# Triangular substitution of a two-stream recurrence: two passes on 64 partitions, or one on 128

## The chip, the cores and the metric

The kernel runs on one core of a Trainium2 chip. The metric is device time in microseconds (us) of one execution. Before the change the median of three runs is 4465.26 us (4459.31 to 4469.98).

## The reference

Two blocks of a network run one after the other over 1024 tokens of 1024 features: a block of two layers (attention and gating, then a mixture of experts, each twice), and a second block with windowed attention, a linear recurrence over time and an MLP. The change touches only the recurrence of the second block. Per head (8 heads of 64 features) and per direction (forward and backward), with a state `S` of 64 by 64:

```python
def step(S, inp):
    r_t, w_t, kk_t, b_t, k_t, v_t = inp
    sa = jnp.einsum('bhvk,bhk->bhv', S, -kk_t)
    S = S * w_t[:, :, None, :] + sa[..., None] * b_t[:, :, None, :] + v_t[..., None] * k_t[:, :, None, :]
    y = jnp.einsum('bhvk,bhk->bhv', S, r_t) if emit else None
    return S, y

S, ys = lax.scan(step, S0, xs, reverse=reverse)
...
for d, rev in enumerate((False, True)):
    S_ctx, yc_d = wkv7_scan(S0, r_c, dec_c, kk_c, b_c, k_c, v_c, rev, update_ctx)   # 256 context tokens
    _, y_d = wkv7_scan(S_ctx, r_l, dec_l, kk_l, b_l, k_l, v_l, rev, True)           # 1024 tokens
    y_lat.append(y_d)
```

The outputs of both directions are added, normalised per head, and merged with the attention branch by two gates; an MLP follows.

## The kernel before

**The recurrence in chunks.** The kernel does not go token by token. It takes chunks of 64 tokens (`C = 64`). Inside a chunk the dependence of tokens on each other is a strictly triangular matrix `A` of 64 by 64 per head and direction, and the chunk needs `(I - A)^-1`. Two chunks of each direction make a group; there are 10 groups (2 over the context, 8 over the tokens). The 8 heads are cut into two streams of four heads (class `Stream`, `hs` = 0 and 1). So one stream in one group has 2 directions x 2 chunks x 4 heads = 16 matrices.

**One group of one stream, before.**
1. `ahead` loads the decayed operands (`AR`, `BKf`; `prepare`, L1866), multiplies them with each other on PE (`pairs`, L1890), masks the products into `MS` on DVE (L1892) and stores the triangles into DRAM as `A_d` (L1898, four stores).
2. `blocks` (L1924) reads back the 16 by 16 blocks on the diagonal of the 16 matrices, four each, so 64 blocks, one per partition (`NL`, L1929). It inverts them by substitution: for n = 1 to 15 one multiplication (L1936) and one reduction (L1938) on DVE, each on 64 partitions by at most 225 elements, each needing the one before. The result goes to DRAM twice, as it is and transposed (`X_d<-XL`, `X_d<-XC`, L1943).
3. `levels` loads the inverses back among zeros, by halves of the partitions (`XX`, `XT`, four loads, L1950), joins the blocks of 16 to 32 and to 64 by small matmuls (`invert`, L1969, L1979) and forms what the values add (`products`, L1920).
4. `finish` makes two steps (`step`, L2011): previous state in, outputs and next state out. From group n = 4 of the tokens on it also calls `output` (L2075), which normalises, transposes (L2105) and stores a finished tile.

So the blocks of 16 go through DRAM twice: `MS` to `A_d` to `NL`, then `XL`, `XC` to `X_d` to `XX`, `XT`. A set of blocks is one pass through step 2; before there are 20 sets (10 groups x 2 streams).

**What runs beside it.** `others` (L1310) yields the window's attention (tiles `wQ`, `wK`, `wP`) and the gates (`gh`, `gw`, products `psA<-gh..,gw..`, L138), piece by piece; `SHARES` says how many pieces follow each group. The recurrence is emitted with priority (`HP = 5000`). A scheduler then fixes one order of instructions per engine, and the engines run these orders as written: an instruction that waits holds all that stand behind it on its engine. All loads and stores of the recurrence go over the SP queue; the gates' loads go over POOL's. What comes after the recurrence is `merge` (tiles `yr`, `ya`).

**Order between the streams.** Before, the loop over the groups goes stream by stream: `ahead` of the next group, `finish` of this one, `levels` of the next one for stream 0, then all three for stream 1. The tiles of `blocks` and of `output` share buffers: `yg` stands in the buffer of `NL` and `XC` (tag `NX`), `yv` and `yrL` in that of `LL`, `ysq` and `yrH` in that of `prod`.

Of the kernel before, what the change touches and what calls it, by code (L numbers as in the profile page):

```python
# [43 lines left out]
class K:  # L44
    """Engines, pools and the few operations that every phase uses."""
# [14 lines left out]
    def after(s, eng):  # L60
        """Work to be queued behind the last instruction of an engine so far."""
        todo = s.nc.cur_bb.bb.instructions
        return s.tc.issue_after(next(x for x in reversed(todo) if x.engine == eng.engine))
# [13 lines left out]
    def banks(s, es, **n):  # L77
        """The eight banks of PSUM, by what they are for, until es closes."""
        old = dict(s.ps)
        s.count += 1  # L80
        p = s.pool(es, f"ps{s.count}", 1, space=PSUM)
        s.ps.update({tag: (p, m) for tag, m in n.items()})

        def back():
            s.ps = old

        es.callback(back)
# [20 lines left out]
    # float32 as the sum of two float32r parts, exact  # L108
# [9 lines left out]
    def row_max(s, pool, todo, mx):  # L118
        """Largest of scores + mask by rows, one column of mx each."""
# [5 lines left out]
    def to_rows(s, pool, cols, n, *dst):  # L125
        """The negatives of columns, one after the other in rows of partition 64."""
# [13 lines left out]
    def weights(s, raw, ring, src, shape, leng=None, queue=None):  # L140
        """A block of weights, loaded and split."""
# [11 lines left out]
    def rstd(s, ss, n, scale, eps, name):  # L153
        """(ss * scale + eps) ** -0.5, few elements per partition."""
# [6 lines left out]
    def bcast(s, pool, ap, n, name, parts=128, **kw):  # L161
        """A row of n values in DRAM on every partition."""
# [5 lines left out]
    def norm_pair(s, pool, xs, gb, outs, eps=EPS, gb2=None):  # L168
        """Two token tiles normalised over their 1024 features and scaled by gb (plus gb2)."""
# [11 lines left out]
    def transpose4(s, src, n=4):  # L181
        """Four [128, 128] blocks of a token tile, transposed into one PSUM bank."""
# [5 lines left out]
    def to_hT(s, src, hH, hL, t):  # L188
        """A token tile [128, 1024] into features by tokens, split."""
# [12 lines left out]
# ---------------------------------------------------------------- even mixer  # L202
# [4 lines left out]
def even_mixer(k, es_out, x_d, w, mod_d):  # L207
    """x_d: DRAM [1024, 1024]. w: DRAM inputs. Returns the output projection and what it takes. The second
    block's modulation goes by the way."""
# [42 lines left out]
def proj_tile(k, hH, hL, W, t, n):  # L252
    """h of token tile t times a block of weights given in chunks of two k-tiles."""
# [74 lines left out]
def even_project(k, es, w, raw, ring, hH, hL, q_d, k_d, v_d):  # L328
    """Queries, keys and values, rotated, in their two parts: q_d, k_d [part, head, feature, token], v_d [part, head,
    token, feature]."""  # L330
# [36 lines left out]
NQ = 4  # heads whose operands are on chip at a time  # L367
# [31 lines left out]
def even_head(k, p2, mb, mc, me, h, slot, q_d, k_d, v_d, a_d, r_d):  # L399
# [13 lines left out]
    # values, by tokens shifted by half a tile and by residue classes of 4  # L413
# [12 lines left out]
    with k.tc.high_priority(offset=HP):  # L426
        # row maxima of both key sets
# [28 lines left out]
    def attend():  # L456
# [21 lines left out]
        # band of 64 tokens to either side  # L478
# [3 lines left out]
        def pv(b, c, v, P):  # L482
            # one accumulation group per bank: what is not yet written is overwritten
# [25 lines left out]
        # dilations 4 and 16, within the residue classes of 4  # L509
# [16 lines left out]
def normalise(k, p2, O, r_row, dst, shape=None, more=None):  # L526
    """Rows 0..63 of O over its row 64 into DRAM. more adds to the row, spread over the partitions."""
# [12 lines left out]
class OutProj:  # L540
    """x + a @ w_out by token tiles; a: features by tokens in DRAM, one tile of 128 features each."""
# [40 lines left out]
# ---------------------------------------------------------------- mixture of experts  # L582
# [5 lines left out]
class Moe:  # L588
    """Expert choice over the tokens of x1; x_d gathers x1 and what the experts add to it."""

    def __init__(s, k, es, i, w, x_d):
# [8 lines left out]
        # the router takes the tokens before their norm: its weights by the norm's  # L600
# [38 lines left out]
    def rank(s, x, last):  # L639
        """The best of every expert so far and these: in order, but for the last time."""  # L640
# [9 lines left out]
        if s.best is not None:  # L650
            # the best of two lists: the one against the other from its end; then sorted
# [14 lines left out]
    def choose(s):  # L666
        """Which slot of which expert a token takes: those above the last of the best by their order, then the
        first of its equals."""
        k, p = s.k, s.p1
        # token number and gate in parts that bfloat16 carries exactly  # L670
# [19 lines left out]
        # how many up to a token, and how many above in all  # L690
# [16 lines left out]
    def gather(s, p, e):  # L707
        """The tokens of an expert, their numbers and gates."""
# [18 lines left out]
    def experts(s):  # L727
        k, w, i = s.k, s.w, s.i
        s.es.close()
        with ExitStack() as es:  # L730
# [11 lines left out]
            # in the order of use: the first products of an expert go ahead of the last of the expert before  # L742
# [65 lines left out]
# ---------------------------------------------------------------- odd mixer  # L808
# [31 lines left out]
def odd_mixer(k, es_out, x_d, w):  # L840
    """x_d: DRAM [1024, 1024]. w: DRAM inputs. Returns the output projection and what it takes."""
    a_d = [k.dram.tile([128, T], F32, name=f"a_do{i}") for i in range(8)]
    r_d = k.dram.tile([16, T], F32, name="r_d1")
    # operands of the attentions in their two parts, features by tokens, by heads or pairs of heads
# [25 lines left out]
def odd_proj(k, es, x_d, w, d):  # L870
# [23 lines left out]
    # ranks: queries, keys and values, rotary keys  # L894
# [27 lines left out]
    def heads(x, n, g, r, t):  # L922
        """Norms and rotations of n heads of a token tile."""
# [8 lines left out]
    def split_rows(src, dst, half, m):  # L932
        """Four token tiles' columns src(t) as features by tokens, split, into dst[part]."""
# [50 lines left out]
    # from the ranks to the heads  # L984
# [39 lines left out]
def odd_attention(k, es, d, a_d, r_d):  # L1024
# [13 lines left out]
    def head(n, h):  # L1038
# [25 lines left out]
        # row maxima of the scores, negated, into a row of the queries' operand  # L1064
# [41 lines left out]
# ---------------------------------------------------------------- second block  # L1106

TC = 256  # context tokens
C = 64  # tokens of a chunk of the recurrence
# [687 lines left out]
class Stream:  # L1797
# [32 lines left out]
    def ahead(s, ctx, n):  # L1830
# [5 lines left out]
        for i in range(2):  # L1836
            s.pairs(B, i)
# [631 lines left out]
```

## Time and profile before

| | before |
|---|---|
| median of 3 runs, us | 4465.26 (4459.31 to 4469.98) |
| span of the profiled execution, us | 4467.4 |
| PE busy, share of the span | 89% |
| DVE busy | 66% |
| ACT busy | 41% |
| POOL busy | 25% |
| first substitution to last one (L1936, L1938), us | 2781.7 to 3451.0 |

The span runs from the first to the last instruction of one profiled execution; it lies between the runs' times, and no other time of that execution is given. PE is TensorE, DVE VectorE, ACT ScalarE, POOL GpSimd, SP the queue that issues most DMAs. A busy PE is not a PE at its peak: the records of matmuls overlap. The recurrence stands in the stretch from 2760 to 3560 us.

### The profile page before, as it was taken

How to read it: one execution, taken by the hardware profiler on the slowest of the kernel's cores; microseconds unless marked ns; L12 is line 12 of the kernel's file. 1: busy time of each engine (PE TensorE's matmuls, PEld its weight loads, DVE VectorE, ACT ScalarE, POOL GpSimd, SP SyncE). 2: the span in 40 equal slices, each digit the busy share in tenths (PEclk: the TensorE clock that was granted, in tenths of full speed). 3: DMA queues.
4: the chain of work that ended last, by engine and by line, in shares of the span. 5: the costliest groups of instructions: out<-in, count | busy, mean ns of one | idle time of the engine just before them, and what ended most of it. 6: DMA issues, size and time to landing. Idle time of an engine off the chain costs nothing. (4 is left out here: it accounts for less than half of the span.)

```text
span 4467.4 us, 65652 instructions
## 1 busy us (share of the span) xinstructions
PE 3963.4 (89%) x24208; PEld 3233.3 (72%) x24208; DVE 2938.6 (66%) x5925; ACT 1815.5 (41%) x3066; POOL 1109.1 (25%) x1069
## 2 busy tenths in 40 slices
PE   7898995897978999689948997999988899999998
PEld 7797884775855666567737776777777678888887
DVE  8656658896678875879866793766677565332334
ACT  3223332675447775257634452333333432212212
POOL 2211212121213433112133363222244511101101
PEclk9998997999989999889968998989998999999999
DMA  5758435898267543569933446555756662111112
GB/s 163 228 170 187 110 112 186 304 367 279 82 189 176 116 102 93 188 238 365 329 111 118 148 148 181 138 142 137 166 145 147 190 210 88 57 48 48 49 55 85
DMA packets 568286, 714.12 MB, mean 160 GB/s; under 512 B 243636, under 2 KB 355332, under 8 KB 567964
## 3 DMA queue, kind: packets, MB, share of 16 engines
q1 hardware_dynamic: 467788, 510.50, 37.3%
q0 software_dynamic: 42480, 144.62, 11.9%
q10 hardware_dynamic: 57696, 54.80, 3.8%
q8 instruction: 191, 3.13, 0.3%
q14 instruction: 131, 1.07, 0.1%
HBM read 555.84 MB, written 153.53 MB: 159 GB/s over the span
## 5 line engine op out<-in xcount | busy, mean ns | idle before, releaser
L116 DVE TENSOR_TENSOR w_l<-w_raw,w_h 128x2048 fp32r<-128x2048 f32 (+5 forms) x336 | 592.2, 1769 | 194.1 <-ACT w_h L111 192.9
L111 ACT ACTIVATE w_h<-w_raw 128x2048 fp32r<-128x2048 f32 (+4 forms) x344 | 507.2, 1487 | 437.4 <-PE psO L138 254.5
L138 PE MATMUL psA<-w_h,hH 128*128 128x256 f32 (+3 forms) x896 | 292.6, 330 | 28.9 <-ACT w_h L111 13.7
L138 PE MATMUL psA<-w_l,hH 128*128 128x256 f32 (+3 forms) x896 | 292.6, 327 | 1.9 <-DVE w_l L116 1.7
L138 PE MATMUL psA<-w_h,hL 128*128 128x256 f32 (+3 forms) x896 | 291.3, 326 | 0.0
L116 POOL TENSOR_TENSOR uL<-relu,uH 128x512 fp32r<-128x512 f32 x64 | 82.6, 1291 | 571.9 <-ACT uH L111 571.9
L138 PE MATMUL psA<-w_h,xH 128*128 128x512 f32 x512 | 208.5, 409 | 11.6 <-ACT xH L111 8.8
L138 PE MATMUL psA<-w_l,xH 128*128 128x512 f32 x512 | 211.1, 412 | 7.1 <-DVE w_l L116 6.9
L138 PE MATMUL psA<-w_h,xL 128*128 128x512 f32 x512 | 206.1, 404 | 4.3 <-DVE xL L116 4.3
L138 PEld LDWEIGHTS psA<-w_h,hH 128*128 128x128 f32 x896 | 174.5, 196 | 41.6 <-ACT w_h L111 15.1
L2287 DVE TENSOR_TENSOR relu<-relu 128x512 f32<-128x512 f32 x64 | 44.3, 693 | 238.2 <-ACT relu L2286 238.2
L116 DVE TENSOR_TENSOR PL<-P,PH 128x512 fp32r<-128x512 f32 x192 | 171.1, 903 | 27.3 <-ACT PH L111 27.1
L138 PEld LDWEIGHTS psA<-w_l,hH 128*128 128x128 f32 x896 | 175.3, 196 | 10.4 <-DVE w_l L116 4.6
L138 PE MATMUL psA<-ghH,gwH 128*128 128x256 f32 x512 | 169.6, 331 | 14.5 <-DMA ghH<-hs_d 5.0
L138 PEld LDWEIGHTS psA<-w_h,hL 128*128 128x128 f32 x896 | 175.1, 195 | 5.3 <-issue 2.6
L805 POOL DMA_INDIRECT x_d<-yo,idx x32 | 69.8, 2182 | 421.5 <-ACT yo L804 417.5
L111 ACT ACTIVATE gwH<-gw 128x256 fp32r<-128x256 f32 x256 | 103.3, 414 | 163.1 <-PE psA L138 121.0
L138 PE MATMUL psA<-ghH,gwL 128*128 128x256 f32 x512 | 161.2, 315 | 1.3 <-POOL gwL L116 1.0
L138 PE MATMUL psA<-ghL,gwH 128*128 128x256 f32 x512 | 160.4, 313 | 0.0
L116 POOL TENSOR_TENSOR gwL<-gw,gwH 128x256 fp32r<-128x256 f32 x128 | 97.5, 765 | 248.3 <-ACT gwH L111 207.5
L111 ACT ACTIVATE PH<-P 128x512 fp32r<-128x512 f32 x256 | 154.5, 629 | 6.5 <-POOL PL L116 1.3
L116 POOL TENSOR_TENSOR PL<-P,PH 128x512 fp32r<-128x512 f32 x64 | 90.9, 1420 | 231.2 <-ACT PH L111 178.2
(654 smaller groups left out, 11896.8 us busy)
## 6 DMA issues: line engine op xcount, KB each, us to landing
w_raw<-in_moe_w_gate_dram SPq DMA_DIRECT2D x64, 1024.0 KB
w_raw<-in_moe_w_up_dram SPq DMA_DIRECT2D x64, 1024.0 KB
w_raw<-in_moe_w_down_dram SPq DMA_DIRECT2D x64, 1024.0 KB
gw<-in_w_in_t_dram POOLq DMA_DIRECT2D x64, 512.0 KB, 5.5
wada<-in_w_ada_dram POOLq DMA_DIRECT2D x48, 512.0 KB, 5.8
w_raw<-in_w_mlp_up_dram SPq DMA_DIRECT2D x16, 1024.0 KB
w_raw<-in_w_mlp_down_dram SPq DMA_DIRECT2D x16, 1024.0 KB
AR<-ar_d SPq DMA_DIRECT2D x40, 256.0 KB
```

Of the source, the lines that this page charges most:

```text
L111: s.a.activation(h, x, AF.Copy)
L116: (eng or s.v).tensor_tensor(l, x, f(h), op=ALU.subtract)
L138: s.t.matmul(ps, a, b, start=first and i == 0, stop=last and i == n - 1)
L805: k.g.indirect_dma_start(out=s.x_d[:, :], out_offset=off, in_=y, in_offset=None, compute_op=ALU.add)
L2287: k.v.tensor_tensor(a, a, a, op=ALU.mult)
```

## The change

Both streams' blocks become one set. `A_d` and `X_d` are now one DRAM tensor for both streams (32 and 64 matrices), `NL`, `LL`, `prod`, `XL` and `XC` have 128 partitions, and `blocks` moves from `Stream` to `Rwkv` and runs once a group: 10 sets instead of 20. To have both streams' triangles ready, the loop goes phase by phase: `prepare` and `pairs` of both streams, `blocks`, `finish` of both, `levels` of both. `output` no longer shares buffers with `blocks`; it has its own. In the changed file the lines of the recurrence stand a few lines lower (`NL` L1812, `LL` L1814, `prod` L1819, `XL` L1821, `XC` L1823, `X_d` L1825, `MS` L1919, `A_d` L1925, `XX` and `XT` L1956).

```diff
     with k.tc.high_priority(offset=HP):
-        G = [x.ahead(*groups[0]) for x in R.streams]
-        for g, x in zip(G, R.streams):
-            x.levels(g)
+        new = R.ahead(*groups[0])
+        R.levels(new)
     for n in range(10):
         with k.tc.high_priority(offset=HP):
-            for i, x in enumerate(R.streams):
-                g = G[i]
-                if n < 9:
-                    G[i] = x.ahead(*groups[n + 1])
-                x.finish(g, yr_d)
-                if n < 9:
-                    x.levels(G[i])
+            G = new
+            if n < 9:
+                new = R.ahead(*groups[n + 1])
+            R.finish(G, yr_d)
+            if n < 9:
+                R.levels(new)
...
 class Rwkv:
+    def ahead(s, ctx, n):
+        last = 1 if ctx else 7
+        gs = (n, last - n)
+        G = [dict(ctx=ctx, n=n, gs=gs, B=[x.prepare(d, ctx, gs[d]) for d in range(2)]) for x in s.streams]
+        for g, x in zip(G, s.streams):
+            for i in range(2):
+                x.pairs(g["B"], i)
+        s.blocks()
+        return G
+    def levels(s, G):
+        for g, x in zip(G, s.streams):
+            x.levels(g)
+    def finish(s, G, yr_d):
+        for g, x in zip(G, s.streams):
+            x.finish(g, yr_d)
+    def blocks(s):
+        k = s.k
+        NL = s.q.tile([128, 16, 16], F32, name="NL", tag="NX")
+        k.d.dma_start(NL, diagonal(s.A_d))
+        LL = s.q.tile([128, 16, 16], F32, name="LL")
+        k.v.tensor_tensor(LL, NL, NL.rearrange("p i j -> p j i"), op=ALU.add)
+        X = s.X
+        prod = s.q.tile([128, 256], F32, name="prod")
+        for n in range(1, 16):
+            pv = prod[:, :n * n].rearrange("p (c j) -> p c j", c=n)
+            k.v.tensor_tensor(pv, X[:, 0:n, 0:n].rearrange("p j c -> p c j"),
+                              LL[:, n, None, 0:n].to_broadcast([128, n, n]), op=ALU.mult)
+            k.v.tensor_reduce(X[:, n, 0:n], pv, op=ALU.add, axis=AX.X)
+        XC = s.q.tile([128, 16, 16], F32, name="XC", tag="NX")
+        k.v.tensor_copy(XC, X.rearrange("p i j -> p j i"))
+        for i, x in enumerate((X, XC)):
+            k.d.dma_start(diagonal(s.X_d, 32 * i), x)
...
 def diagonal(x, lo=0):
-    x = x[lo:lo + 16]
-    return bass.AP(tensor=x.tensor, offset=x.offset, ap=[[16 * 65, 64], [64, 16], [1, 16]])
+    x = x[lo:lo + 32]
+    return bass.AP(tensor=x.tensor, offset=x.offset, ap=[[16 * 65, 128], [64, 16], [1, 16]])
...
 class Stream:
-            k.d.dma_start(matrices(s.A_d, 8 * d + 4 * c, 4), MS[rds[d], d, :, 0:64])
+            k.d.dma_start(matrices(s.R.A_d, 16 * s.hs + 8 * d + 4 * c, 4), MS[rds[d], d, :, 0:64])
...
-        for d, t, i in ((0, XX, 0), (1, XT, 1), (0, XT, 2), (1, XX, 3)):
-            k.d.dma_start(t[64 * d:64 * d + 64], matrices(s.X_d, 8 * i, 8))
+        for d, t, i in ((0, XX, 0), (1, XT, 0), (0, XT, 1), (1, XX, 1)):
+            k.d.dma_start(t[64 * d:64 * d + 64], matrices(s.R.X_d, 32 * i + 16 * s.hs + 8 * d, 8))
...
-        v = s.q.tile([128, 256], F32, name="yv", tag="LL")
+        v = s.q.tile([128, 256], F32, name="yv")
-        g = s.q.tile([128, 256], F32, name="yg", tag="NX")
+        g = s.q.tile([128, 256], F32, name="yg")
-        sq = s.q.tile([128, 256], F32, name="ysq", tag="prod")
+        sq = s.q.tile([128, 256], F32, name="ysq")
```

The engines' orders differ from the first piece of the recurrence on. PE and ACT have the same number of instructions as before; DVE has 320 fewer, SP 30 fewer, POOL 2 fewer.

The SP queue in the middle of the recurrence, before: the end of one set's triangles, the other stream's inverses going out, and their way back.

```order
L1898 DMA A_d_24955<-MS_29453 64x4x64 x2
L1943 DMA X_d_24950<-XL 64x16x16
L1943 DMA X_d_24950<-XC 64x16x16
L1929 DMA NL<-A_d_24955 64x16x16
L1950 DMA XX<-X_d_24950 64x8x64
L1950 DMA XT<-X_d_24950 64x8x64 x2
L1950 DMA XX<-X_d_24950 64x8x64
L1874 DMA AR_30391<-ar_d_20664 128x2x256
```

The SP queue in the same part, now: one set for both streams, with the next operands and values (`AR`, `SV`) between the loads of the two streams' inverses.

```order
L1812 DMA NL<-A_d 128x16x16
L1941 DMA SV_30614<-u_v 64x256
L1941 DMA SV_30616<-u_v 64x256
L1941 DMA SV_30727<-u_v 64x256
L1941 DMA SV_30729<-u_v 64x256
L1825 DMA X_d<-XL 128x16x16
L1825 DMA X_d<-XC 128x16x16
L1901 DMA AR_31226<-ar_d_20663 128x2x256
L1956 DMA XX<-X_d 64x8x64
L1956 DMA XT<-X_d 64x8x64 x2
L1956 DMA XX<-X_d 64x8x64
L1901 DMA AR_31230<-ar_d_20664 128x2x256
```

Before, one stream's blocks came in (`NL`) while the other's inverses went out; now the stores and loads of both stand in one place, and an `AR` load, which waits for PE to have done with the old operands, stands between the stores of the inverses and their loads.

DVE, before: the last steps of one stream's substitution, the other stream's masks, and then that stream's set.

```order
L1938 TENSOR_REDUCE XL<-prod 64x15
L2030 TENSOR_TENSOR RV_29695<-psP_30784,RV_29695 128x256
L1940 COPY XC<-XL 64x256
L1892 TENSOR_TENSOR MS_30719<-psQ,ms 128x4x128
L116 TENSOR_TENSOR gwL<-gw,gwH 128x256
L2052 TENSOR_TENSOR S<-psP_30545,Sh_24970 64x256 x2
L2024 TENSOR_TENSOR Sh_24969<-S,dt 64x4x64 x2
L116 TENSOR_TENSOR gwL<-gw,gwH 128x256
L1931 TENSOR_TENSOR LL<-NL 64x256
```

DVE now, from the last masks of both streams to the first steps of the common set.

```order
L2058 TENSOR_TENSOR S<-psP_29173,Sh_24966 64x256 x2
L1496 TENSOR_TENSOR wP<-psA,mk 128x512
L2030 TENSOR_TENSOR Sh_24965<-S,dt 64x4x64 x2
L1919 TENSOR_TENSOR MS_29045<-psQ,ms 128x4x128
L2058 TENSOR_TENSOR S<-psP_29271,Sh_24977 64x256 x2
L2030 TENSOR_TENSOR Sh_24976<-S,dt 64x4x64 x2
L1496 TENSOR_TENSOR wP<-psA,mk 128x512
L1814 TENSOR_TENSOR LL<-NL 128x256
L1819 TENSOR_TENSOR prod<-XL,LL 128x1
L1821 TENSOR_REDUCE XL<-prod 128x1
```

The shapes have 128 partitions and the same free sizes; between the last mask and `LL`, which waits for the blocks to come back from DRAM, stand six instructions before and five now.

PE at the end of the recurrence, before: the last transposes of a finished tile (`c_ident,Y`) between products of the gates.

```order
L138 MATMUL psA<-ghL,gwH 128x256
L138 MATMUL psA<-ghH,gwL 128x256
L2105 MATMUL psP_35422<-c_ident,Y_35274 128x128 x2
L138 MATMUL psA<-ghH,gwH 128x256
L138 MATMUL psA<-ghL,gwH 128x256
```

PE at the last but one finished tile, now.

```order
L138 MATMUL psA<-ghL,gwH 128x256
L138 MATMUL psA<-ghH,gwL 128x256
L2111 MATMUL psP_34999<-c_ident,Y_34881 128x128 x2
L138 MATMUL psA<-yrH_35327,w_h 128x512
L138 MATMUL psA<-yrL_35328,w_h 128x512
```

Before, gates are left over when the recurrence ends; now they are used up at the last but one tile, and the merge's first products stand behind it.

## Rows read from the trace of the kernel before

**Rows 1.** Stretches: from:to, length, busy PE, PEld, DVE, ACT, POOL, PEclk, DMA.
```profile
2760.00:3560.00 800.00, 717.35 (x8260) 576.22 (x8259) 549.44 (x1543) 297.41 (x732) 275.97 (x354) 0.90 0.61 150
3290.00:3360.00 70.00, 65.93 (x799) 51.36 (x799) 57.80 (x167) 25.42 (x65) 31.39 (x40) 0.93 0.62 144
```
**Rows 2.** Chain of waits over 2760 to 3560, shares by line.
```profile
by line: PE psA L138 15.2%; DMA XX<-X_d 8.4%; PE psQ L1890 6.3%; DMA NL<-A_d 5.9%; PE psL L1969 4.1%; DMA X_d<-XL 3.9%; issue 3.8%; DVE prod L1936 3.6%; PE psM L1502 2.9%; DMA A_d<-MS 2.7%; DVE XL L1938 2.6%; DMA ghH<-hs_d 2.5%; SPq L1950 2
```
**Rows 3.** PE's waits, 2760 to 3560: us in total, times, longest us.
```profile
PE psL L1969 <- DMA XX<-X_d: 31.9, 21, 5.0
PE psQ L1901 <- DVE MS L1892: 7.6, 8, 3.1
PE psP L2028 <- DVE Y L2071: 7.0, 2, 3.5
PE psP L2060 <- DVE S L2052: 6.1, 6, 3.4
...
PE psA L138 <- DVE wmx L1478: 3.6, 2, 3.3
```
**Rows 4.** Groups of instructions, DVE, 2760 to 3560: count, busy us, mean ns, idle before.
```profile
L1936 DVE TENSOR_TENSOR prod<-XL,LL 64x36 f32<-64x36 f32 (+4 forms) x300 | 99.0, 331 | 6.6
...
L1938 DVE TENSOR_REDUCE XL<-prod 64x6 f32<-64x36 f32 (+4 forms) x300 | 67.8, 228 | 6.7 <-DVE prod L1936 0.2
...
L1997 DVE TENSOR_TENSOR XT<-psL,XT 64x256 f32<-64x256 f32 x40 | 16.8, 420 | 10.2 <-PE psL L1969 9.4
...
L2030 DVE TENSOR_TENSOR RV<-psP,RV 128x256 f32<-128x256 f32 x38 | 15.8, 416 | 8.7 <-ACT RV L1921 4.5 <-PE psP L2028 3.9
...
L1931 DVE TENSOR_TENSOR LL<-NL 64x256 f32<-64x256 f32 x20 | 13.9, 693 | 38.9 <-DMA NL<-A_d 38.8
...
L1940 DVE COPY XC<-XL 64x256 f32<-64x256 f32 x20 | 9.2, 459 | 0.3
```
**Rows 5.** Chain of waits, the DRAM hops of two sets: start us, us, what.
```profile
3018.36 2.29 DMA A_d<-MS
3020.67 4.90 DMA NL<-A_d
...
3062.97 2.60 DMA X_d<-XL
3065.58 4.77 DMA XX<-X_d
```
**Rows 6.** Timeline of PE around one wait: start, us, engine, line, operation, [idle before].
```profile
3144.43 0.42 PE L1969 MATMUL psL<-XX,MS 64*64 64x32 f32 x2 [5.02 <-DMA XX<-X_d]
...
3154.86 0.41 PE L138 MATMUL psA<-ghL,gwH 128*128 128x256 f32 x1
3155.07 0.41 PE L138 MATMUL psA<-ghH,gwL 128*128 128x256 f32 x1
...
3156.26 0.28 PE L138 MATMUL psA<-ghH,gwL 128*128 128x256 f32 x1
3156.38 0.28 PE L138 MATMUL psA<-ghH,gwH 128*128 128x256 f32 x1
```
**Rows 7.** Timeline of DVE around one load of the blocks.
```profile
3025.59 0.59 DVE L1931 TENSOR_TENSOR LL<-NL 64x256 f32<-64x256 f32 x1 [5.20 <-DMA NL<-A_d]
```
**Rows 8.** Stretches of 6 us around these two waits, columns as in Rows 1.
```profile
3020.00:3026.00 6.00, 6.00 (x85) 5.06 (x84) 0.81 (x2) 3.22 (x8) 0.82 (x2) 1.00 0.50 125
3139.00:3145.00 6.00, 0.98 (x20) 0.78 (x16) 0.00 (x0) 0.86 (x2) 2.34 (x5) 0.79 1.09 211
```

More of the change, by code (lines that the diff above doesn't have):

```diff
@@ L1769, in open @@
         s.lnb = k.bcast(p1, w["lnx_b_2"][0], 512, "lnb")
+        s.A_d = k.dram.tile([32, PM], F32, name="A_d")
+        s.X_d = k.dram.tile([64, PM], F32, name="X_d")
         with ExitStack() as es1:
@@ L1772, in open @@
             k.g.memset(z, 0.0)
-            s.streams = [Stream(s, hs, z) for hs in range(2)]
+            for i in range(8):
+                k.d.dma_start(s.X_d[8 * i:8 * i + 8].rearrange("u (a c) -> (u a) c", a=16), z)
+        s.streams = [Stream(s, hs) for hs in range(2)]
         for x in s.streams:
             x.open(es)
+        s.q = k.pool(es, "rw5", 1)
+        s.X = s.q.tile([128, 16, 16], F32, name="XL")
+        k.g.memset(s.X, 0.0)
+        k.g.memset(s.X.rearrange("p a b -> p (a b)")[:, 0:256:17], 1.0)
         for x in s.streams:
             x.q = k.pool(es, f"rw3{x.hs}", 1)
+    def ahead(s, ctx, n):
[30 more added lines that the diff above has]
+            k.d.dma_start(diagonal(s.X_d, 32 * i), x)
 PM = 65 * 64
@@ L1791, in diagonal, with __init__ @@
 def diagonal(x, lo=0):
-    x = x[lo:lo + 16]
-    return bass.AP(tensor=x.tensor, offset=x.offset, ap=[[16 * 65, 64], [64, 16], [1, 16]])
+    x = x[lo:lo + 32]
+    return bass.AP(tensor=x.tensor, offset=x.offset, ap=[[16 * 65, 128], [64, 16], [1, 16]])
 class Stream:
-    def __init__(s, R, hs, zero):
-        k = s.k = R.k
+    def __init__(s, R, hs):
+        s.k = R.k
         s.R, s.hs = R, hs
@@ L1804, in __init__ @@
         s.y_d = [None] * 8
-        s.A_d = k.dram.tile([16, PM], F32, name=f"A_d{hs}")
-        s.X_d = k.dram.tile([32, PM], F32, name=f"X_d{hs}")
-        for i in range(4):
-            k.d.dma_start(s.X_d[8 * i:8 * i + 8].rearrange("u (a c) -> (u a) c", a=16), zero)
     def open(s, es):
@@ L1814, in open @@
         s.p = k.pool(es, f"rw2{s.hs}", 1)
-        s.X = s.p.tile([64, 16, 16], F32, name="XL")
-        k.g.memset(s.X, 0.0)
         s.W = [s.p.tile([128, 8, 64], F32, name=f"W{i}") for i in range(2)]
@@ L1821, in open @@
             k.g.memset(x, 0.0)
-        k.g.memset(s.X.rearrange("p a b -> p (a b)")[:, 0:256:17], 1.0)
     def P(s):
@@ L1828, in L @@
         return s.k.bank(f"L{s.hs}")
-    def ahead(s, ctx, n):
-        k = s.k
-        last = 1 if ctx else 7
-        gs = (n, last - n)
-        B = [s.prepare(d, ctx, gs[d]) for d in range(2)]
-        for i in range(2):
-            s.pairs(B, i)
-        s.blocks()
-        return dict(ctx=ctx, n=n, gs=gs, B=B)
     def levels(s, G):
@@ L1922, in products @@
         return RV
-    def blocks(s):
-        k, p = s.k, s.p
-        NL = s.q.tile([64, 16, 16], F32, name="NL", tag="NX")
-        k.d.dma_start(NL, diagonal(s.A_d))
-        LL = s.q.tile([64, 16, 16], F32, name="LL", tag="LL")
-        k.v.tensor_tensor(LL, NL, NL.rearrange("p i j -> p j i"), op=ALU.add)
-        X = s.X
-        prod = s.q.tile([64, 256], F32, name="prod", tag="prod")
-        for n in range(1, 16):
-            pv = prod[:, :n * n].rearrange("p (c j) -> p c j", c=n)
-            k.v.tensor_tensor(pv, X[:, 0:n, 0:n].rearrange("p j c -> p c j"),
-                              LL[:, n, None, 0:n].to_broadcast([64, n, n]), op=ALU.mult)
-            k.v.tensor_reduce(X[:, n, 0:n], pv, op=ALU.add, axis=AX.X)
-        XC = s.q.tile([64, 16, 16], F32, name="XC", tag="NX")
-        k.v.tensor_copy(XC, X.rearrange("p i j -> p j i"))
-        for i, x in enumerate((X, XC)):
-            k.d.dma_start(diagonal(s.X_d, 16 * i), x)
     def load(s):
@@ L2105, in output @@
             k.t.transpose(pt[:, 128 * j:128 * j + 128], y[:, 128 * j:128 * j + 128], k.ident)
-        H, L = (s.q.tile([128, 256], F32R, name="yr" + a, tag=t_) for a, t_ in (("H", "prod"), ("L", "LL")))
+        H, L = (s.q.tile([128, 256], F32R, name="yr" + a, tag=t_) for a, t_ in (("H", "ysq"), ("L", "yv")))
         k.hi(H, pt)
```

## The prediction

> **What bounds the kernel now.** I read the page's slices first, then the stretch of the recurrence. From 2760 to 3560 us PE is busy for 717 of 800 us and DVE for 549 [rows 1]: PE is the fuller engine, with 83 us idle, and a granted clock of 0.90. DVE is 69% full over the stretch and 83% in its fullest part, 57.8 of 70 us [rows 1]. So the stage is not a plain chain: the gates and the window's attention fill the time in which the recurrence waits. The chain of waits of the stretch confirms it: its largest single share is the gates' and scores' products (15.2%), then the four DRAM hops of the blocks (8.4, 5.9, 3.9 and 2.7%), and only 6.2% is the substitution itself on DVE [rows 2].
>
> What ends PE's idle time says what the stage can win. PE waits 31.9 us in 21 waits for the inverses to land (`XX`), and 24.3 us in the four largest rows that name DVE (7.6, 7.0, 6.1 and 3.6) [rows 3].
>
> [...]
>
> **The change, part by part.**
>
> *DVE's instructions.* Ten sets take the place of twenty. The multiplications go from 300 to 150, the reductions too, the additions `LL` and the copies `XC` from 20 to 10. By mean duration that is 99.0/2 + 67.8/2 + 13.9/2 + 9.2/2 = 95 us of DVE work less [rows 4], if an instruction on 128 partitions takes as long as one on 64. Two rows bear on that: an addition of 256 elements from PSUM takes 420 ns on 64 partitions and 416 ns on 128 [rows 4]. DVE falls from 549 to about 455 us of the stretch.
>
> How much of the 95 us does PE see? DVE isn't the fullest engine, so no more than its waits for DVE, 24.3 us, and no less than none. I take 40%, 10 us: if waiting behind a queue goes as busy over idle share, it falls from 69/31 = 2.2 to 57/43 = 1.3.
>
> *The inverses' way back.* Before, 20 sets cost PE 31.9 us, 1.6 us a set [rows 3]. Now 10 sets. A set's stores `X_d` hold twice as many pieces; the step for one took 2.60 us [rows 5]. No row shows a 128-partition store of this form, so the extra lies between nothing and another 2.60 us; I take 0.8, nearer to nothing, since after it the loads of four tiles of twice that size in all landed within 4.77 us [rows 5], so time does not go with bytes. Ten sets of 2.4 us make 24 us: 8 us less. The ends: 10 sets without any wait give 31.9 us less; 10 sets at the longest wait seen, 5.0, give 18 us more.
>
> [...] A block's row here is 16 floats, 64 bytes, and the changed transfers have twice as many such pieces. [...]
>
> *The blocks' way in.* DVE waits 38.8 us for `NL` over 20 sets [rows 4], up to 5.20 us in the one shown [rows 7]. With five instructions between the last mask and `LL`, it will wait again, in half as many sets: I expect 27 us (10 sets at 1.9 plus the same 0.8), and price it at nothing on PE, because its cover can be seen: during that wait DVE did 0.81 us of work in 6 us and PE was busy for all 6 [rows 8], with products already fed. If that cover is gone, it costs up to 10 x 5.2 = 52 us, which is the slower rival below.
>
> *The queue of SP.* Thirty transfers go. The loads of the second stream's inverses stand behind `AR` loads that wait for PE, and behind the first stream's. I price that at nothing: the second stream's inversion comes after the first's on PE, whose 64 small products and masks lie between. The buffers of `output` no longer hold up `NL` in the last five groups; a gain that I don't count, since PE has fill there.
>
> *PE's own work* is unchanged: same instructions, other order. At the end no gates are left beside the last tile, but the merge's products stand there instead.
>
> *The clock.* Idle time falls by 10 + 8 = 18 us. [...]
>
> *Sum.* 10 + 8 + 8 = 26 us less than the profiled span of 4467.4, so 4441. That span is 2 us above the median of the runs shown, 4465.3, and the runs lie within 4459 to 4470. Against the median the forecast is 4439 us.
>
> **The rivals.**
>
> *No change.* The 95 us are off the path. For it: the rows name the substitution hardly at all as what PE waits for; PE's waits for DVE name masks, states and outputs [rows 3], which stay. Then the DVE term falls to 2 us, ten waits for inverses at 3.2 us add up to what twenty at 1.6 were, and the clock gives nothing: 4463. It differs from the forecast in whether DVE's shorter queue brings the masks and states forward.
>
> *Slower: both streams stand still at once.* Before, while one stream's blocks went through DRAM, the other stream had matmuls and masks in the queues. Now both streams wait in the same place: DVE at `LL`, with both streams' next work behind it, then PE at the first inverse. The price for a set is 5.2 us for the one stop [rows 7] and 5.0 for the other [rows 3], 102 us in ten sets, in place of 31.9 + 24.3 = 56 us: 46 us more, and with a quarter of it for the clock 57 more: 4522. It decides from the point where a set stops PE for more than 5.6 us in all. For it: the chain's four hops are 21% of the stretch [rows 2], and now stand in one line for both streams. Against: PE kept busy through just such a wait [rows 8], and the fill is the same.
>
> [...]
>
> *The tail.* The recurrence ends later against the gates, and its last tile has no gates beside it; 142 products of the gates and the window stood behind the last step's, at 0.12 us each [rows 6] some 17 us of cover. If the merge's loads don't fill it, the forecast loses these 17: 4455.
>
> **How the numbers follow.** The forecast has 0.47 (its own range 4415 to 4455), no change 0.18, slower 0.20, much faster 0.09, the tail 0.06. A difference of 0.2%, 9 us, is about what a measurement of this kernel tells from none. The forecast and much faster are over that; so is half of the tail; the rest of it goes to no change: faster 0.59, same 0.21, slower 0.20. The range takes in the forecast, no change, the tail, the upper part of much faster and the nearer half of slower: 4400 to 4485.
>
> **What would show it.** Right: 150 multiplications and 150 reductions on 128 partitions with the same mean of 331 and 228 ns; DVE busy for about 455 us in the stretch; PE's waits for `XX` at about 24 us in some ten waits; PE's waits that name masks, states and `Y` smaller by a third; a granted clock above 0.90. Wrong: DVE's work gone and PE's idle time of 83 us still there (no change), or PE idle in a stretch in which DVE sits at `LL` (slower). If the store `X_d` takes near 5 us the price of the pieces was wrong.

## Result and profile after

The changed kernel takes 4508.97 us (median of 4 runs, 4500.36 to 4521.72), the kernel before 4464.64 us beside it (4 runs): ratio 1.0089, 95% interval 1.0067 to 1.0111. By the medians that is 44 us slower (by the ratio 40) where 26 us faster was forecast, and it lies outside the range. The profiled execution of the changed kernel has a span of 4520.0 us, 52.6 us over that of before.

Up to the recurrence both kernels run alike, and the loss is complete after it: the first `relu` of the MLP starts at 3818.9 us instead of 3766.6. First the stretch of rows 1 in the changed kernel, then a wait of DVE and one of PE (columns as in [rows 1]):

```profile
2760.00:3560.00 800.00, 692.78 (x7939) 560.58 (x7938) 435.26 (x1149) 276.17 (x680) 248.04 (x323) 0.86 0.57 134
...
3072.00:3078.00 6.00, 6.00 (x65) 4.84 (x63) 0.02 (x1) 1.59 (x4) 0.72 (x1) 1.00 0.53 101
3107.00:3113.00 6.00, 0.00 (x1) 0.00 (x0) 0.00 (x0) 0.00 (x0) 1.48 (x3) 0.79 1.08 219
```

DVE is busy for 114 us less than in [rows 1], 95 of them the substitution's; of the rest, part is work that now stands behind 3560 us. PE is nevertheless idle for 107 us instead of 83, and the granted clock fell from 0.90 to 0.86, which is 32 us in 800. The two overlap: read in stretches of 1 us, 9 of the 32 us lie in idle time, so that here PE loses 24.6 us by standing still and 23.5 by its clock. The two short rows answer to [rows 8]: while DVE waits for blocks, PE is busy for all 6.00 us; while PE waits for inverses, nothing on PE, DVE or ACT goes on, and the DMA engines are full (1.08).

The whole way from 2720 us to the first `relu`, before and now:

```profile
2720.00:3766.60 1046.60, 937.93 (x9234) 755.85 (x9235) 697.73 (x1762) 366.53 (x855) 320.69 (x408) 0.91 0.60 156
```
```profile
2720.00:3818.90 1098.90, 954.63 (x9245) 770.38 (x9246) 619.85 (x1456) 369.43 (x859) 317.73 (x407) 0.88 0.58 149
```

PE is idle for 144.3 us instead of 108.7, 35.6 more, and in the same stretches of 1 us the clock costs a busy PE some 24 us more. That is 60 us for a loss of 52; the profile does not resolve the difference.

The groups of DVE's instructions in the same stretch (columns as in [rows 4]):

```profile
L1819 DVE TENSOR_TENSOR prod<-XL,LL 128x1 f32<-128x1 f32 (+4 forms) x150 | 48.1, 321 | 3.7
L1821 DVE TENSOR_REDUCE XL<-prod 128x1 f32<-128x1 f32 (+4 forms) x150 | 35.5, 237 | 3.7
...
L1814 DVE TENSOR_TENSOR LL<-NL 128x256 f32<-128x256 f32 x10 | 6.5, 655 | 27.8 <-DMA NL<-A_d 27.8
L1823 DVE COPY XC<-XL 128x256 f32<-128x256 f32 x10 | 4.8, 482 | 0.3
```

The instructions took about as long on 128 partitions as on 64: 321 ns on the mean against 331, 237 against 228 [rows 4]. And PE's waits in the stretch (columns as in [rows 3]):

```profile
PE psL L1975 <- DMA XX<-X_d: 45.9, 16, 7.3
PE psQ L1917 <- DMA AR<-ar_d: 8.2, 5, 4.4
PE psA L1467 <- DMA wQ<-wq_d: 5.8, 2, 3.2
PE psL L1985 <- DVE XX L2005: 4.6, 2, 3.5
...
PE psQ L1917 <- DVE MS L1919: 4.5, 4, 2.1
PE psP L2034 <- DVE Y L2077: 4.1, 2, 3.0
...
PE psQ L1928 <- DVE MS L1919: 3.5, 3, 1.4
PE psA L138 <- DVE wmx L1469: 3.2, 4, 2.5
PE psA L1467 <- DVE wmx L1476: 3.0, 1, 3.0
...
PE psA L138 <- DVE wmx L1476: 1.9, 2, 1.0
...
PE psP L2066 <- DVE S L2058: 1.8, 1, 1.8
```

Three more rows of the kernel before, to set beside them:

```profile
PE psQ L1890 <- DMA AR<-ar_d: 3.7, 1, 3.7
...
PE psQ L1890 <- DVE MS L1892: 3.4, 3, 1.8
...
PE psA L1469 <- DMA wQ<-wq_d: 1.3, 3, 0.8
```

The four rows that name DVE in [rows 3] fell from 24.3 to 11.3 us (3.5, 4.1, 1.8 and 1.9; the old line L1478 of `wmx` is now L1476). But other rows that name DVE grew, and all of them together went only from 33.5 to 32.2 us. The wait for the inverses did not fall to 24 us but rose from 31.9 to 45.9, in 16 waits instead of 21. The waits for `AR` and for the attention's `wQ` rose too, and all of PE's waits for transfers went from 41.9 to 64.5 us: 22.6 of the 24.6 us by which PE stands still longer.

How one set's inverses come home, in SP's queue (start, duration, line, transfer). DVE's copy `XC` started at 3095.03 and took 0.38 us:

```profile
3095.43 0.36 SPq L1825 DMA_DIRECT2D X_d<-XC  x1
3097.64 0.59 SPq L1925 DMA_DIRECT2D A_d<-MS  x1
3098.32 0.60 SPq L1956 DMA_DIRECT2D XX<-X_d  x1
3098.97 1.34 SPq L1956 DMA_DIRECT2D XT<-X_d  x2
3100.36 1.31 SPq L1956 DMA_DIRECT2D XX<-X_d  x2
3101.71 4.06 SPq L1956 DMA_DIRECT2D XT<-X_d  x2
3105.81 2.90 SPq L1956 DMA_DIRECT2D XX<-X_d  x1
```

PE around it (columns as in [rows 6]):

```profile
3102.08 0.30 PE L1975 MATMUL psL<-XX,MS 64*64 64x32 f32 x2 [0.45 <-DMA XX<-X_d]
...
3105.86 0.28 PE L138 MATMUL psA<-ghH,gwH 128*128 128x256 f32 x1
...
3113.02 2.20 PE L1975 MATMUL psL<-XX,MS 64*64 64x32 f32 x32 [6.01 <-DMA XX<-X_d]
...
3117.10 0.41 PE L138 MATMUL psA<-ghH,gwH 128*128 128x256 f32 x1
3117.31 0.41 PE L138 MATMUL psA<-ghL,gwH 128*128 128x256 f32 x1
```

One set is stored at once, but it comes home in two portions of four loads. The first stream's is used at 3102.08, 6.7 us after the copy; the second's stands behind it in SP's queue, and PE waits 6.01 us for it until 3113.02. Behind this stop the gates' products start 0.21 us apart, with a granted clock of 0.50 in every us from 3111 to 3130; ahead of it, at 1.00, they start 0.12 us apart from 3103.45 us on. Sorted by stream, the 16 waits of the stretch are nine for first portions, 25.5 us, and seven for second ones, 20.4 us.

The queue is not the only thing in the way. These are the DMA queues from 3107 to 3113 us, while PE stands still (packets, MB, busy share of the 16 engines; `q0` is POOL's queue, `q1` SP's):

```profile
q0 software_dynamic: 317, 1.10, 82.6%
q1 hardware_dynamic: 870, 0.22, 25.1%
```

The loads of the gates and the attention that POOL issued from 3099.96 us on (`gw`, `wK`, `wQ`, `wVA`) take four fifths of the engines, where POOL's queue takes 22% of them over the stretch. Of the 45.9 us, 24.6 are waits in which it takes over 40%; before, it was 7.2 of 31.9. No run moved these loads, so how much of the wait is theirs is not shown.

At the very end PE waits once more, for POOL's last products of `output`, with nothing of the gates left behind it:

```profile
3603.55 0.69 PE L2111 MATMUL psP<-c_ident,Y 128*128 128x128 f32 x2 [10.77 <-POOL Y L2108]
```

### The profile page after: what moved, and what is told of

Read it like the earlier page. It is cut to its first block, busy times and chain, and to the rows that moved or that the text cites. A ratio compares the mean times of both kernels' runs of the same rounds, so it can differ in the third digit from the quotient of the medians.

```text
span 4520.0 us, 65328 instructions
## 1 busy us (share of the span) xinstructions
PE 3970.9 (88%) x24208; PEld 3236.9 (72%) x24208; DVE 2857.8 (63%) x5605; ACT 1816.7 (40%) x3066; POOL 1108.3 (25%) x1067
## 5 line engine op out<-in xcount | busy, mean ns | idle before, releaser
L116 POOL TENSOR_TENSOR uL<-relu,uH 128x512 fp32r<-128x512 f32 x64 | 82.6, 1290 | 570.4 <-ACT uH L111 570.4
```

The source lines that it names most:

```text
L116: (eng or s.v).tensor_tensor(l, x, f(h), op=ALU.subtract)
```

## Experiments

Ratios are against the kernel before in the same group of runs, with 95% intervals. One profiled execution can stand up to 23 us off its kernel's median (4464.77 against 4488.26 in the last run below, 4513.22 against 4494.05 with the streams swapped), so times are compared by ratios, and rows of several profiles together.

**Parts of the change.** *The phases alone, two sets of 64 partitions:*

```diff
-                    for i, x in enumerate(R.streams):
-                        g = G[i]
-                        if n < 9:
-                            G[i] = x.ahead(*groups[n + 1])
+                    old = G
+                    if n < 9:
+                        G = [x.ahead(*groups[n + 1]) for x in R.streams]
+                    for g, x in zip(old, R.streams):
                         x.finish(g, yr_d)
-                        if n < 9:
-                            x.levels(G[i])
+                    if n < 9:
+                        for g, x in zip(G, R.streams):
+                            x.levels(g)
```

> The kernel before, with its two sets of 64 partitions a group, but the loop goes phase by phase (ahead of both streams, finish of both, levels of both). Theory 'in step': the loss of 44 us comes from the order, since both streams now wait for their DRAM hops at the same time; then this kernel is slower than before by at least as much, 4500 to 4560 us, as it also has 95 us more work on DVE than the changed kernel. Theory 'merging': the loss comes from the common set (it waits for the later stream's masks, its transfers have twice as many pieces); then this kernel is within 12 us of before, 4453 to 4477.

4512.18 us, 1.0090 [1.0061, 1.0119]: as "in step" said.

*The merged set, steps and levels stream by stream:*

```diff
-                    R.finish(G, yr_d)
-                    if n < 9:
-                        R.levels(new)
+                    for i, x in enumerate(R.streams):
+                        x.finish(G[i], yr_d)
+                        if n < 9:
+                            x.levels(new[i])
```

> The changed kernel with its common set, but after the set the loop goes stream by stream again: finish of stream 0, levels of stream 0, finish of stream 1, levels of stream 1. Theory 'in step': with the later half of the group staggered again, most of the 44 us come back, 4455 to 4480 us. Theory 'merging': the inverses of both streams still come at one moment and the loss stays, 4500 to 4520 us.

4507.04 us, 1.0081 [1.0057, 1.0106]: as "merging" said.

*The changed kernel, inverses loaded over ACT's queue instead of SP's:*

```diff
-            k.d.dma_start(t[64 * d:64 * d + 64], matrices(s.R.X_d, 32 * i + 16 * s.hs + 8 * d, 8))
+            k.a.dma_start(t[64 * d:64 * d + 64], matrices(s.R.X_d, 32 * i + 16 * s.hs + 8 * d, 8))
```

> The changed kernel with the eight loads of the inverses (XX, XT) issued from ACT's queue instead of SP's, where loads of AR and SV that wait for PE stand ahead of them. Theory 'queue': PE's waits for XX (45.9 us in the changed kernel) fall by half and the time by 30 us or more, to 4465 to 4485. Theory 'in step' or 'merging': the hops' own length sets the waits, XX stays above 35 us and the time within 12 us of 4509; slower if ACT's own work holds the loads up.

4510.82 us, 1.0087 [1.0056, 1.0119]. The wait it was aimed at did fall, from 45.9 us to this, and the time stayed where it was:

```profile
PE psL L1975 <- DMA XX<-X_d: 29.5, 13, 6.8
```

Neither theory had both: "queue" wanted the time back, the others a wait above 35 us. PE's waits that name DVE rose in its place, from 32.2 to 41.8 us.

*The kernel before with every second substitution step left out (the inverses are then not complete):*

```diff
-        for n in range(1, 16):
+        for n in range(1, 16, 2):
```

> The kernel before with 8 of the 15 steps of the substitution (n = 1, 3, 5, ...): it leaves out half of DVE's substitution work (about 80 us of DVE in 20 sets, and 4 us of every set's chain) and changes nothing else in the program; its inverses are therefore not the true ones. Theory 'DVE is off the path' (the no-change rival of the prediction): 4450 to 4470 us. Theory of the prediction (a shorter DVE queue brings masks and states forward): 18 us or more faster, 4425 to 4447.

4516.13 us, 1.0108 [1.0075, 1.0140], above what either theory gave. The four answers do not add up: either half of the change alone cost as much as both, and less DVE work in the kernel before, with no other edit, cost most. What the four share is that the scheduler laid the rows down in another order. So the next runs changed the order alone.

**The order alone.** *The kernel before, two numbers of the fill's shares* (the fill is the pieces of `others` that run beside the recurrence; 170 pieces as before, and the instructions stay the same):

```diff
-SHARES = (30, 30, 25, 25, 20, 10, 10, 10, 5, 5)
+SHARES = (28, 30, 25, 25, 22, 10, 10, 10, 5, 5)
```

> The kernel before with the same instructions; only the pieces of fill handed out after the first and the fifth group of the recurrence differ (28 and 22 for 30 and 20), so that the engines' rows stand in another order from the middle of the stretch on. Theory 'order' (the kernel before owes about 40 us to the one order of rows in which its stops came out few, and any other order of the same work loses them): 4490 to 4515 us. Rival 'content' (the time hangs on the instructions and their waits, an order more or less moves little): 4455 to 4480 us.

4473.44 us, 1.0023 [1.0007, 1.0039].

*The kernel before, its streams the other way round:*

```diff
-                    for i, x in enumerate(R.streams):
+                    for i, x in reversed(list(enumerate(R.streams))):
```

> The kernel before with the same instructions, the second stream's part of each group ahead of the first's, so that the rows stand in another order from the start of the stretch on. Theory 'order': 4490 to 4515 us. Rival 'content': 4455 to 4480 us, as the two streams' work is alike.

4494.05 us, 1.0065 [1.0045, 1.0085]: 29 us from the order of rows. The first of the two lies where "content" put it, the second where "order" did.

*The changed kernel with shares of 28 and 22:*

> The changed kernel with the fill handed out as in the first kernel of this group (28 and 22 for 30 and 20). Theory 'order' with the changed kernel at a usual order: 4495 to 4520 us, a change of either sign by up to 15 us against 4509 us. Rival 'content': within 6 us of 4509 us.

4481.53 us, 1.0035 [1.0019, 1.0052]: 27 us less than the changed kernel as given by the medians, 24 by the ratios, more than either theory allowed. More such pairs, shares of 26 and 24, then of 32 and 18:

> The kernel before with fill shares of 26 and 24 for 30 and 20 after the first and fifth group; nothing but the order of rows differs. Theory 'draw' (each order is a draw: the kernel before lies at the low end of its orders, 4465 of 4465, 4473 and 4494, and the changed kernel at the high end of its own, 4509 of 4482 and 4509): 4468 to 4500 us. Rival 'content' (what the change adds is worth 16 to 44 us in any order): within 10 us of 4465 us, and the changed kernel with the same shares at least 16 us above it.

> The changed kernel with fill shares of 26 and 24 for 30 and 20. Theory 'draw': anywhere from 4465 to 4510 us, and on the mean of the four orders of the changed kernel no more than 15 us above the mean of the four of the kernel before. Rival 'content': 16 to 44 us above the kernel before with the same shares.

> The kernel before with fill shares of 32 and 18 for 30 and 20. Theory 'draw': 4468 to 4500 us. Rival 'content': within 10 us of 4465 us.

> The changed kernel with fill shares of 32 and 18 for 30 and 20. Theory 'draw': anywhere from 4465 to 4510 us. Rival 'content': 16 to 44 us above the kernel before with the same shares.

And the changed kernel with its streams swapped in `pairs`, `levels` and `finish` (the kernel before swaps their loads and blocks as well):

> The changed kernel, the second stream ahead of the first in pairs, levels and steps; beside the kernel before with its streams swapped (4494 us). Theory 'draw' (the change is worth 2 to 8 us, and the rest is the order): 4470 to 4505 us. Rival 'content' (worth 16 us or more): above 4510 us.

| same edit in both | before | changed | difference |
|---|---|---|---|
| as given (30, 20) | 1 | 1.0089 [1.0067, 1.0111] | 0.0089 |
| 28, 22 | 1.0023 [1.0007, 1.0039] | 1.0035 [1.0019, 1.0052] | 0.0012 |
| 26, 24 | 1.0036 [1.0022, 1.0051] | 1.0041 [1.0023, 1.0058] | 0.0005 |
| 32, 18 | 1.0052 [1.0035, 1.0069] | 1.0070 [1.0053, 1.0088] | 0.0018 |
| streams swapped | 1.0065 [1.0045, 1.0085] | 1.0075 [1.0048, 1.0103] | 0.0010 |

In four of five pairs the changed kernel is 0.05 to 0.18% slower, 2 to 8 us, less than a pair's interval; only as given is it 40 us by the ratios. The same edit does not give both kernels the same order, so a pair sets one order of each side by side, and five pairs are few. The kernel before is the fastest of its five orders, the changed kernel as given the slowest of its own. The rival "content" said at least 16 us in every pair and falls; the theory "order" of the first runs, any other order loses 40 us, was too strong as well: 10 to 29 us by the ratios.

Stretches of 900 us, PE to DMA as in [rows 1], of the kernel before with 28 and 22, then swapped:

```profile
2720.00:3620.00 900.00, 788.79 (x8611) 636.59 (x8612) 592.56 (x1629) 327.10 (x791) 306.59 (x393) 0.90 0.61 154
```
```profile
2720.00:3620.00 900.00, 774.87 (x8429) 615.12 (x8430) 564.29 (x1592) 311.67 (x761) 294.45 (x384) 0.86 0.58 144
```

and of the changed kernel as given, then with 28 and 22:

```profile
2720.00:3620.00 900.00, 767.41 (x8422) 619.24 (x8423) 487.49 (x1279) 309.13 (x761) 291.67 (x383) 0.85 0.58 141
```
```profile
2720.00:3620.00 900.00, 771.46 (x8537) 617.08 (x8538) 508.80 (x1298) 319.74 (x779) 298.98 (x388) 0.89 0.61 149
```

The reader is to see that the same instructions give 0.90 or 0.86 in the kernel before, and 0.85 or 0.89 in the changed one. The profiles of the two slow orders share the low clock (0.86 and 0.85), not one wait: the largest rows beside `XX` in the swapped order are these.

```profile
PE psL L1969 <- DMA XX<-X_d: 35.7, 23, 5.3
PE psQ L1890 <- DMA AR<-ar_d: 13.6, 7, 5.0
PE psA L138 <- DMA yrH<-yr_d: 11.0, 1, 11.0
PE psL L1979 <- DVE XL L1938: 9.6, 1, 9.6
```

**The way back, and the balance with the fill.** *The changed kernel with the inverses of the set before, two buffers in turn:*

```diff
-            k.d.dma_start(diagonal(s.X_d, 32 * i), x)
+            k.d.dma_start(diagonal(s.X_ds[s.sets % 2], 32 * i), x)
+        s.sets += 1
...
-            k.d.dma_start(t[64 * d:64 * d + 64], matrices(s.R.X_d, 32 * i + 16 * s.hs + 8 * d, 8))
+            k.d.dma_start(t[64 * d:64 * d + 64], matrices(s.R.X_ds[s.R.sets % 2], 32 * i + 16 * s.hs + 8 * d, 8))
```

> The changed kernel, whose inverses are read from what the set before stored (two buffers in DRAM in turn), so that PE's wait for the way back of the inverses is gone while every instruction and transfer stays; the values are then those of other blocks. The term in dispute is the 45.9 us in which PE stands still ahead of the first product on XX and the low clock behind these stops. Theory 'way back' (this wait and its clock are what the change lost): the 45.9 us and about as much clock again come back in part, 4420 to 4465 us. Rival 'order' (stops move to other places when one kind is taken away): above 4485 us.

4567.65 us, 1.0234 [1.0210, 1.0258]: PE's wait for `XX` cut from 45.9 us to this, and 59 us slower than the changed kernel:

```profile
PE psL L1978 <- DMA XX<-X_d: 16.7, 7, 4.8
```

Its last step's product starts at 3434.0 us instead of 3589.5, with 649 of the gates' 1536 products still to come (24 in the changed kernel, 144 in the one before). *The same, the recurrence preferred less:*

```diff
-HP = 5000
+HP = 800
```

> The changed kernel with the inverses of the set before (the values are those of other blocks; 4568 us with 649 of the 1536 gate products left behind the last step) and the recurrence preferred by 800 instead of 5000 places, which leaves 78 gate products. Theory 'way back' (its stops and their clock cost 50 us or more, and the first try hid this behind the gates left alone): 4400 to 4455 us. Rival 'order' (other stops take their place): 4465 to 4510 us.

4465.54 us, 1.0004 [0.9989, 1.0018]: 102 us less by that number alone, with 78 gate products left. From 3434 to 3650 us, first with 5000, then with 800 (columns as in [rows 1]):

```profile
3434.00:3650.00 216.00, 158.95 (x863) 120.81 (x857) 72.14 (x180) 81.52 (x198) 101.97 (x132) 0.88 0.54 150
```
```profile
3434.00:3650.00 216.00, 197.09 (x1438) 153.18 (x1435) 144.53 (x310) 91.89 (x201) 93.21 (x109) 0.94 0.64 190
```

The gates left alone did not fill PE: it was busy for 159 of 216 us against 197. With both in step, `XX` costs 8.8 us:

```profile
PE psL L1978 <- DMA XX<-X_d: 8.8, 4, 3.5
```

and the whole is no faster than the kernel before: just in the range of "order". It is 14 us (0.0031) under the best order of the changed kernel, and 24 us (0.0054) under the kernel before with 800, which comes next. The changed kernel with 800 and its own way back was not run, so what the way back is worth once the fill keeps step is not shown.

*Half the steps in the kernel before, and the kernel before itself, each with 800:*

> The kernel before with half of the substitution steps left out (every second one, as in the earlier kernel with half the steps, 4516 us) and the recurrence preferred to the fill by 800 instead of 5000 places. In the earlier one the recurrence ran ahead and left 384 of the 1536 gate products behind its last step (144 in the kernel before); here 72 are left. Theory 'balance' (the 47 us were the gates left alone at the end, and less DVE work pays once these are spread): 4425 to 4460 us. Rival 'DVE is off PE's path, orders are draws': 4465 to 4500 us.

> The kernel before, the recurrence preferred by 800 instead of 5000 places: the same instructions, 24 of the 1536 gate products left behind the last step instead of 144. Control of the first. Theory 'balance': the recurrence's own tail is now alone at the end, as in the changed kernel (24 left, too): 4480 to 4510 us. Rival (a draw like the others): 4465 to 4494 us.

4478.08 us, 1.0026 [1.0006, 1.0046], and 4481.15 us, 1.0058 [1.0034, 1.0081]. The kernel with half the steps gained 38 us on its first order (384 gate products left, now 72); it lies in the range of "DVE is off PE's path" and not in that of "balance". Against its control it is 3 us faster by medians, 0.0032 by ratios (14 us, with an interval of about as much): so 57 us less DVE work, in the stretches below, are worth between nothing and half of that:

```profile
2720.00:3620.00 900.00, 806.73 (x8564) 643.17 (x8565) 530.45 (x1357) 324.18 (x786) 304.83 (x391) 0.89 0.60 152
```
```profile
2720.00:3620.00 900.00, 797.35 (x8587) 631.14 (x8588) 587.91 (x1617) 322.77 (x782) 303.87 (x392) 0.90 0.61 153
```

The control can't tell its two theories apart, 4481 lies in both.

**Two more orders.** *The merged set stream by stream, and the phases in step with two sets, each with 26 and 24:*

> The changed kernel with levels and steps stream by stream (4507 us) and the fill's shares of 26 and 24 for 30 and 20. If orders are draws of the same work: 4470 to 4500 us; below 4460 us only if the merged set is worth something that the orders so far have hidden.

> The kernel before with the phases of the changed loop and two sets of 64 partitions, as in the first experiment (4512 us), and the fill's shares of 26 and 24 for 30 and 20. Theory 'draw': 4470 to 4500 us, about as the kernel before with these shares (4485 us). Rival 'in step' (two streams that wait at one time cost 40 us in any order): 4505 to 4525 us.

4489.79 us, 1.0070 [1.0049, 1.0091], and 4488.26 us, 1.0057 [1.0036, 1.0078]. By the ratios the first gave back 5 us of its first order's cost, the second 15; the kernel before with these shares is at 1.0036. So streams in step cost some 9 us here, with an interval of about 12 either way, not 40. No version ran faster than the kernel before.

## Why the prediction was wrong

**DVE's instructions: the work right, its worth on PE wrong.** There are 150 multiplications and reductions at unchanged means, and DVE is at 435 us (455 forecast). Of this PE was to see 10 us, and the sign that was named for it came: PE's waits for masks, states and `Y` fell from 24.1 to 13.9 us. But other rows took their place, so that all rows that name DVE stand at 32.2 us instead of 33.5; over the five pairs they stand at 34.8 instead of 35.6 on the mean. The prediction looked at four rows and not at what PE would wait for next. Half the steps against its control leaves room for more, between nothing and half of 57 us.

**The inverses' way back: mis-sized, with the wrong sign.** "Ten sets of 2.4 us make 24 us": 45.9 in the changed kernel as given. Over the five orders PE's wait for `XX` is 31.9, 32.4, 34.1, 51.5 and 35.7 us before and 45.9, 41.1, 41.5, 41.4 and 48.5 after, 37.1 against 43.7 on the mean: 6.6 us more, where 8 less was forecast. The step counted a stop for a set. But stores are per set and loads still per stream, so there are 20 returns, and the second stands behind the first in SP's queue, which the prediction priced at nothing. As given, the first returns cost 25.5 us, near the 24, and the second ones 20.4. Inverses on ACT's queue took 16 us off this wait, so the queue has a part in it; the loads of POOL, which no term of the prediction has, may have another.

The bigger store was sized about right. From the issue of the first half, `X_d<-XL`, to that of the loads, as in [rows 5], one of the quickest sets before and one of the quickest now took 2.56 and 3.08 us:

```profile
2980.97 0.62 SPq L1943 DMA_DIRECT2D X_d<-XL  x1
2981.74 0.61 SPq L1943 DMA_DIRECT2D X_d<-XC  x1
2983.53 0.59 SPq L1950 DMA_DIRECT2D XX<-X_d  x1
```
```profile
3481.01 0.38 SPq L1825 DMA_DIRECT2D X_d<-XL  x1
3481.73 0.61 SPq L1825 DMA_DIRECT2D X_d<-XC  x1
3484.09 0.60 SPq L1956 DMA_DIRECT2D XX<-X_d  x1
```

Where nothing else stood between them, the four quickest sets before took 2.55 to 2.61 us and the three quickest now 3.01 to 3.16; the mean of all sets is 4.6 us before and 5.2 now. So twice the pieces cost about half a us (0.8 forecast), though the reason given for it was misread: the four loads hold 512 KB, four times the two stores' 128 KB and not twice. A store that takes another 2.60 us, the upper end that the prediction allowed, would have given 5.2 us, an estimate from [rows 5]; the quick sets do not show it. In four of the ten sets the issue of `X_d<-XC` alone lasted 2.48 to 6.21 us with the DMA engines full (0.98 to 1.11), and there pieces and full engines can't be told apart.

**The blocks' way in: right.** 27.8 us at `LL` (27 forecast), and PE busy beside it for 6.00 of 6 us in the wait shown, for 24.9 of 27.8 us in all nine.

**The clock: wrong sign.** 8 us were to come back; 0.86 instead of 0.90 is 32 us lost, 23.5 of them while PE was busy. The 8 us, and the quarter that the slower rival adds for the clock, were the author's estimates, which no run shows. What the profiles show is 24.6 us more idle time beside 23.5 us of clock as given; and in the four stretches of 900 us above, in their order, PE is idle for 111, 125, 133 and 129 us, while the granted clock comes to 90, 126, 135 and 99 us lost, so these show no fixed rate of one to the other.

**PE's own work and the end.** The 10.77 us at 3603.55 are the tail that a rival had at 17 (its sum is 4456, not 4455).

**The sum.** Between the two profiles PE's idle time grew by 35.6 us: 14.0 are waits for `XX`, 9.0 those for `AR` and `wQ`, 10.8 the tail, and waits for DVE gave back 1.3. The clock took some 24 us more. But this is the account of one order against one order, and two steps failed.

The first are the gains: 10 us for DVE, 8 for the inverses, 8 for the clock. On the mean of the five pairs PE's waits for DVE shrank by 0.8 us and those for `XX` grew by 6.6, so the 18 us less idle time, beside which the 8 us for the clock were put, did not come. Over the four pairs other than the one as given the change by itself is worth 0.0011, 5 us slower, with an interval of about 6 us either way worked out from theirs (0.0027, 12 us, with all five). That is the rival "no change", put at 0.18, and its reason, that DVE is off the path, fits the rows.

The second is "PE's own work is unchanged: same instructions, other order": it priced the other order at nothing, while the kernel before, with the same instructions, ran up to 29 us slower in another order, more than the sum's 26. By the pairs the order makes some 35 of the 40 us as given. No rival was made for the order.

**The slower rival** came near in time (4522), and in cause only in part. PE did stand longer at the inverses, but DVE's stop at `LL` left PE busy, and both streams in step ran at 4488 us in a second order. Its own point was 5.6 us of PE's stops in a set, waits for `XX` and the four rows of DVE together: 45.9 and 11.3 us in ten sets are 5.7, on the point and far from the 10.2 that it reckoned with.

**What stays open.** Why the order as given is so low in clock (0.85 against 0.89 with 28 and 22, over 900 us): no one wait separates it from that other order, which has `XX` at 41.1 us. How much of the wait for `XX` is SP's queue and how much the loads of POOL on the same DMA engines was not measured, and is an untested rival; nor were the own buffers of `output` tried by themselves.

## What to carry to other kernels

Where a scheduler lays down the rows and a second stream of work fills the first one's waits, run the kernel before in a few other orders of the same instructions (a share, a swap) before pricing an edit: their spread, 29 us here, is the least that a forecast's range must hold, and an edit under it is judged by pairs. Of a wait that is removed ask what it kept in step: cutting PE's longest wait from 45.9 to 16.7 us cost 59 us while the fill was left behind, and with the preference set anew 102 us came back. Add up all rows that name an engine before pricing what a lighter load on it gives: four of them fell by 13 us here and all of them by 1.3. Count a round trip by its loads as well as by its stores, and look at what else fills the DMA engines while it is under way.

## What the runs showed of the hardware

Moving eight loads a set from SP's queue to ACT's cut PE's wait for them from 45.9 to 29.5 us without moving the time (4510.82 against 4508.97 us). Twice as many pieces of 64 bytes in the stores `X_d` took 3.01 to 3.16 us to the loads in the quickest sets, against 2.55 to 2.61 us. In 6 us in which PE waited for its inverses on SP's queue, POOL's queue took 82.6% of the DMA engines' time and SP's 25.1%. DVE's multiplications of 1 to 225 elements took 321 ns on the mean on 128 partitions and 331 ns on 64.
